# One load of the first tokens, issued as two transfers of 16 and 112 partitions

## The chip, the cores and the metric

The kernel runs on one core of a Trainium2 chip. The metric is the device time of one execution in microseconds. The kernel before took 180.99 us (median of three runs, 180.95 to 182.24 us).

A core has five instruction streams that run side by side and wait for each other on semaphores: TensorE (PE, the matrix multiplier), VectorE (DVE), ScalarE (ACT), GpSimd (POOL) and SyncE (SP). Transfers between the device memory and the on-chip memory are issued by SyncE, ScalarE or GpSimd, each on a queue of its own, and are carried out by 16 DMA engines that all queues share.

## The reference

Eight experts, each with its own 256 tokens, two weight matrices and two biases. All inputs are float32.

```
x: (8, 256, 512)   w1: (8, 512, 2048)   w2: (8, 2048, 512)   b1: (8, 2048)   b2: (8, 512)

h   = relu(matmul(x, w1) + b1)      # per expert: 256 x 2048
out = matmul(h, w2) + b2            # per expert: 256 x 512, float32
```

The weights are 4 MB for each of the 16 matrices in float32, and every one is used for 256 tokens only.

## The kernel before

**Data.** The kernel computes in float16. GpSimd's queue loads the weights and converts them on the way (`load`, line 88, called from `load_w1` and `load_w2`): one transfer for a matrix, except for the `w2` of the last two experts, which come in two halves. The tokens of experts 2 and 3 come in one transfer and those of experts 4 to 7 in another, on the same queue. Weights have room for three experts (`NW = 3`), so a later load waits until TensorE has finished with the one whose place it takes: for `s_ph` (first products of an expert done) or `s_po` (second products done).

**The tokens of experts 0 and 1** come another way. SyncE loads each as float32 into a tensor of its own, `x32[0]` and `x32[1]`, 128 partitions of 1024 elements (lines 131 and 132). Each partition holds two consecutive tokens, so a load is contiguous in device memory. VectorE casts expert 0 to float16 (line 133) and turns it with 32x32 block transposes into `xT` (function `transposes`, lines 121 and 124); ScalarE casts expert 1 (line 135). The two float32 tensors serve again at the end, as the places where the results of the last two experts are collected before SyncE stores them (line 246).

**Order before the section.** The lines up to 135 stand before a section that is synchronised by hand (line 138). In that first part the waits come from the framework, which tracks what each instruction reads and writes: the cast in line 133 waits for all transfers into `x32[0]`. SyncE's instructions of the first part are its x loads; in the section it first waits for what the first part leaves open. The issue of the first weights by GpSimd does not wait for any x load.

**The section.** SyncE is the gatekeeper (`go`, lines 240 to 242): it waits for the transposed tokens (`s_xT`) and for the landing of a weight load, and then raises `s_go`, on which TensorE waits. TensorE runs a loop of 11 steps (line 282). Step s computes the first product of expert s (line 292, 128 matmuls into four PSUM buffers, `ph`) and the second product of expert s - 3 (lines 319 and 309, into `po`). The page counts part of the matmuls of a group as one record. ScalarE adds the bias and applies the relu to each `ph` (line 226). For that it needs `b1T`, the transposed bias, which VectorE makes from rows that ScalarE has loaded (lines 129 and 191), between the transposes of expert 0 and those of expert 1. VectorE and ScalarE evict `po` (line 206).

**GpSimd's order** is: w1 of expert 0, b2, w1 of expert 1, tokens of experts 2 and 3, w1 of expert 2, w1 of expert 3, w2 of expert 0, tokens of experts 4 to 7, and from then on w1 and w2 in turn, w2 three experts behind. After the last weights come the stores of experts 0 to 3 and of 4 and 5; those of experts 6 and 7 are SyncE's.

Of the kernel before, what the change touches and what calls it, by code (L numbers as in the profile page):

```python
# [10 lines left out]
def kernel(  # L11
# [12 lines left out]
    nc = tc.nc  # L24
# [6 lines left out]
    P = 128  # L31
    nTB = T // P
# [15 lines left out]
    def sbuf(name, shape, dtype):  # L48
        return ctx.enter_context(nc.sbuf_tensor(name, shape, dtype))
# [14 lines left out]
    x32 = [sbuf(f"x32_{e}", [P, nTB, H], fp32) for e in range(2)]  # L64
# [39 lines left out]
    def transposes(e):  # L104
# [23 lines left out]
    tc.keep_in_program_order(nc.scalar.activation(out=warm[:], in_=ones1[:], func=relu))  # L128
    tc.keep_in_program_order(nc.scalar.dma_start(
        out=b1_rows[:], in_=b1.rearrange("e (b i) -> (e b) i", b=nB)))  # L130
    for e in range(2):
        nc.sync.dma_start(out=x32[e][:], in_=x[e].rearrange("(p tb) h -> p tb h", tb=nTB))
    nc.vector.tensor_copy(out=x16[0][0][:], in_=x32[0][:])  # L133
    transposes(0)
    tc.keep_in_program_order(nc.scalar.copy(out=x16[1][0][:], in_=x32[1][:]))  # L135
# [29 lines left out]
    def flush(first):  # L165
        n = GROUPS[first]
        for tb in range(nTB):
# [6 lines left out]
         in_=b2.rearrange("e h -> (e h)").rearrange("(o f) -> o f", o=1))  # L174
# [15 lines left out]
    for b in range(nB):  # L190
        turned = nc.vector.transpose(  # L191
            out=b1T[b * B : (b + 1) * B, nB - 1 - b : nB - 1 - b + nJ * B],
            in_=b1_rows[:].rearrange("r (i j) -> r j i", j=nJ),
# [23 lines left out]
    for s in range(E + LAG):  # L217
        if s < E:
# [3 lines left out]
            for j in range(nJ):  # L222
# [4 lines left out]
                    out=mine.rearrange("p (tb j k i) -> p j tb k i", tb=nTB, j=nJ, k=split)[:, j],  # L227
                    in_=ph[:, j % NPH, 0:T].rearrange("p (tb i k) -> p tb k i", tb=nTB, k=split),
# [19 lines left out]
    for s in range(E + LAG):  # L248
# [5 lines left out]
        e = s - LAG  # L254
# [112 lines left out]
```

## Time and profile before

| | |
|---|---|
| median of three runs | 180.99 us (180.95 to 182.24) |
| profiled execution, whole time | 181.05 us |
| its span, first to last instruction | 179.3 us |
| mean granted TensorE clock | 0.973 |
| busy: TensorE / VectorE / ScalarE / GpSimd | 133.7 / 86.8 / 75.5 / 12.5 us |
| read from device memory / written to it | 71.39 / 4.19 MB |
| the two x loads of SyncE, issue to landing | 3.4 and 4.5 us |
| first matmul | 16.14 us |
| last eviction begins | 173.13 us |

All times within an execution are counted from the start of the span. A row of a timeline gives the start, the duration, the engine and source line, the tile written and the one read, the number of instructions taken together, and in brackets the idle time before it with what ended it. "SPq" and "PEq" are the sequencers of SyncE and TensorE: issues and waits that are not counted as busy time. The queues are q0 (GpSimd), q1 (SyncE) and q10 (ScalarE). A transfer's time is from its issue to the moment when its semaphore shows that it has landed.

### The profile page before, as it was taken

How to read it: one execution, taken by the hardware profiler on the slowest of the kernel's cores; microseconds unless marked ns; L12 is line 12 of the kernel's file. 1: busy time of each engine (PE TensorE's matmuls, PEld its weight loads, DVE VectorE, ACT ScalarE, POOL GpSimd, SP SyncE). 2: the span in 40 equal slices, each digit the busy share in tenths (PEclk: the TensorE clock that was granted, in tenths of full speed). 3: DMA queues.
4: the chain of work that ended last, by engine and by line, in shares of the span. 5: the costliest groups of instructions: out<-in, count | busy, mean ns of one | idle time of the engine just before them, and what ended most of it. 6: DMA issues, size and time to landing. Idle time of an engine off the chain costs nothing. (4 is left out here: it accounts for less than half of the span.)

```text
span 179.3 us, 3015 instructions
## 1 busy us (share of the span) xinstructions
PE 133.7 (75%) x784; PEld 92.9 (52%) x784; DVE 86.8 (48%) x124; ACT 75.5 (42%) x153; POOL 12.5 (7%) x27
## 2 busy tenths in 40 slices
PE   0003979868699880998978896889699896999960
PEld 0003868858589330794468544874298333443420
DVE  0989938576000299998089906992320002031010
ACT  3201776757687113483097506780487111021010
POOL 6000011020200100001010001000200003010000
PEclk9999999999999998589999999999999999999996
DMA  5999999998999998999999999999989989999996
GB/s 209 273 194 218 234 194 218 234 219 190 236 223 190 230 230 190 223 234 216 194 234 223 194 227 230 208 205 234 219 190 234 223 190 223 210 212 221 316 424 261
DMA packets 3826, 40.46 MB, mean 226 GB/s; under 512 B 448, under 2 KB 464, under 8 KB 1136
## 3 DMA queue, kind: packets, MB, share of 16 engines
q0 software_dynamic: 3200, 38.28, 96.7%
q1 hardware_dynamic: 576, 2.10, 3.0%
q10 hardware_dynamic: 48, 0.07, 0.1%
q14 instruction: 2, 0.02, 0.0%
HBM read 71.39 MB, written 4.19 MB: 422 GB/s over the span
## 5 line engine op out<-in xcount | busy, mean ns | idle before, releaser
L292 PE MATMUL ph<-xT,w_sb 128*128 x512 | 72.2, 302 | 33.3 <-PEq L277 30.4
L292 PEld LDWEIGHTS ph<-xT,w_sb 128*128 x512 | 66.5, 145 | 40.1 <-issue 31.3
L226 ACT ACTIVATE hT<-ph,b1T 128x256 f16<-128x256 f32 x128 | 60.2, 474 | 33.4 <-PE ph L292 29.9
L124 DVE STREAM_TRANSPOSE xT<-x 32x256 f16<-32x256 f16 (+1 forms) x64 | 52.7, 893 | 25.2 <-DMA x<-in_x_dram 22.0
L309 PE MATMUL po<-w_sb,hT 128*128 x256 | 56.7, 379 | 2.2 <-issue 2.2
L309 PEld LDWEIGHTS po<-w_sb,hT 128*128 x256 | 24.9, 97 | 33.1 <-issue 7.1
L206 DVE COPY out<-po 32x512 f32<-32x512 f32 (+1 forms) x20 | 13.7, 687 | 42.9 <-PE po L309 42.6
L206 ACT COPY out<-po 32x512 f32<-32x512 f32 (+1 forms) x20 | 11.6, 578 | 46.0 <-PE po L309 45.8
L88 POOL DMA_DIRECT2D w_sb<-in_w_dram x18 | 9.7, 544 | 137.4 <-PE po L309 71.2
L121 DVE STREAM_TRANSPOSE xT<-x 32x256 f16<-32x256 f16 x32 | 14.0, 436 | 0.5
L206 DVE COPY x<-po 128x512 f32<-128x512 f32 x2 | 1.4, 692 | 14.0 <-PE po L309 14.0
L319 PE MATMUL po<-b_sb,ones 1*128 x16 | 4.8, 378 | 3.9 <-issue 2.5
L206 ACT COPY x<-po 128x512 f32<-128x512 f32 x2 | 1.2, 586 | 14.3 <-PE po L309 14.3
L319 PEld LDWEIGHTS po<-b_sb,ones 1*128 1x128 f16 x16 | 1.4, 90 | 6.6 <-issue 6.3
L191 DVE STREAM_TRANSPOSE b1T<-b_rows 32x512 f32<-32x512 f32 x4 | 4.1, 1023 | 0.5 <-issue 0.5
L135 ACT CAST x<-x 128x1024 f16<-128x1024 f32 x1 | 1.0, 1044 | 3.3 <-DMA x<-in_x_dram 3.3
L133 DVE CAST x<-x 128x1024 f16<-128x1024 f32 x1 | 0.7, 694 | 3.1 <-DMA x<-in_x_dram 3.1
L88 POOL DMA_DIRECT2D out_dram<-out x2 | 1.1, 538 | 9.5 <-DVE out L206 9.5
L128 ACT ACT_TABLE_LOAD x1 | 1.3, 1283 | 0.7 <-PEq L351 0.7
L88 POOL DMA_DIRECT2D x<-in_x_dram x2 | 1.1, 550 | 0.0
L127 DVE MEMSET ones<- 1x128 f16 x1 | 0.2, 165 | 0.9 <-PEq L351 0.9
L88 POOL DMA_DIRECT2D b_sb<-in_b_dram x1 | 0.5, 509 | 0.0
(5 smaller groups left out, 0.7 us busy)
## 6 DMA issues: line engine op xcount, KB each, us to landing
w_sb<-in_w_dram POOLq DMA_DIRECT2D x14, 2048.0 KB, 41.2
w_sb<-in_w_dram POOLq DMA_DIRECT2D x4, 1024.0 KB, 22.5
out_dram<-out POOLq DMA_DIRECT2D x1, 2048.0 KB, 25.1
x<-in_x_dram SPq DMA_DIRECT2D x2, 512.0 KB, 4.0
x<-in_x_dram POOLq DMA_DIRECT2D x1, 1024.0 KB, 34.5
out_dram<-out POOLq DMA_DIRECT2D x1, 1024.0 KB, 18.1
out_dram<-x SPq DMA_DIRECT2D x2, 512.0 KB, 7.0
x<-in_x_dram POOLq DMA_DIRECT2D x1, 512.0 KB, 24.5
```

Source lines behind the costliest of these rows:

```text
L88: engine.dma_start(**kw).then_inc(landed[key], 16)
L121: last = nc.vector.transpose(out=dst[:, :, g, :, 0, :], in_=block[:, :, :, 0, :])
L124: last = nc.vector.transpose(out=dst[:, tb, g], in_=block[:, tb])
L128: tc.keep_in_program_order(nc.scalar.activation(out=warm[:], in_=ones1[:], func=relu))
L133: nc.vector.tensor_copy(out=x16[0][0][:], in_=x32[0][:])
L135: tc.keep_in_program_order(nc.scalar.copy(out=x16[1][0][:], in_=x32[1][:]))
L191: turned = nc.vector.transpose(out=b1T[b * B : (b + 1) * B, nB - 1 - b : nB - 1 - b + nJ * B], in_=b1_rows[:].rearrange("r (i j) -> r j i" ...
L206: last = copy(out=results[e][at : at + rows, k * nTB + tb, :], in_=po[k * rows : (k + 1) * rows, bank : bank + H])
L226: nc.scalar.activation(out=mine.rearrange("p (tb j k i) -> p j tb k i", tb=nTB, j=nJ, k=split)[:, j], in_=ph[:, j % NPH, 0:T].rearrange("p ...
L292: last = nc.tensor.matmul(ph[:, j % NPH, 0:T], w1_sb[:, bass.ds(w_from + (kc * M + j), P, nJ)], xT[:, bass.ds(x_at + kc * T, T)], start=(k ...
L309: return nc.tensor.matmul(banks[tb], hT[:, bass.ds(h_from + (tb * nJ + j) * P, P)], w2_sb[:, bass.ds(w2_from + j * H, H)], start=False, st ...
L319: nc.tensor.matmul(banks[tb], ones1[:], b2_sb[:, bass.ds(s * H, H)], start=True, stop=False)
```

## The change

SyncE's first load is issued as two transfers: partitions 0 to 15 of `x32[0]`, then partitions 16 to 127. Both go on SyncE's queue, one after the other, ahead of the load of expert 1, which stays as it was. A partition's data is 4 KB, so the first transfer carries 64 KB and the second 448 KB. Nothing else in the source is changed; the cast in line 133 reads the whole tensor and so depends on both.

```diff
@@ -128,8 +128,8 @@
     tc.keep_in_program_order(nc.scalar.activation(out=warm[:], in_=ones1[:], func=relu))
     tc.keep_in_program_order(nc.scalar.dma_start(
         out=b1_rows[:], in_=b1.rearrange("e (b i) -> (e b) i", b=nB)))
-    for e in range(2):
-        nc.sync.dma_start(out=x32[e][:], in_=x[e].rearrange("(p tb) h -> p tb h", tb=nTB))
+    for e, p0, p1 in ((0, 0, 16), (0, 16, P), (1, 0, P)):
+        nc.sync.dma_start(out=x32[e][p0:p1], in_=x[e].rearrange("(p tb) h -> p tb h", tb=nTB)[p0:p1])
     nc.vector.tensor_copy(out=x16[0][0][:], in_=x32[0][:])
     transposes(0)
     tc.keep_in_program_order(nc.scalar.copy(out=x16[1][0][:], in_=x32[1][:]))
```

## The prediction

> **What bounds the kernel now.** I read the page's head and its parts 2 and 3 first: which engine is busy all the time?
>
> ```profile
> span 179.3 us, 3015 instructions
> DMA  5999999998999998999999999999989989999996
> q0 software_dynamic: 3200, 38.28, 96.7%
> q1 hardware_dynamic: 576, 2.10, 3.0%
> ```
>
> The DMA engines are at nine tenths in nearly every slice, and GpSimd's queue (q0) alone holds them for 96.7% of the span. SyncE's queue (q1), which the change touches, holds them for 3.0%: two x loads at the start, two stores at the end. Next the table by stretches (share of the 16 DMA engines and GB/s are the last two columns; six stretches from 6 to 168 us were asked, the first of these rows is the second of them), SyncE's waits between 131 and 150 us (total, times, longest), and the semaphore line of `go`.
>
> ```profile
> 20.00:50.00 30.00, 24.33 (x180) 22.69 (x178) 16.56 (x41) 20.97 (x46) 3.71 (x7) 1.00 1.02 216
> 140.00:168.00 28.00, 25.48 (x114) 10.97 (x113) 3.44 (x5) 2.90 (x5) 2.13 (x4) 1.00 1.01 212
> SPq L241 <- DMA w_sb<-in_w_dram: 19.2, 2, 9.7
> L242 SPq EVENT_SEMAPHORE  x18: 17/28/7361, 15.5 to 168.6; - x18
> ```
>
> The DMA share is 1.0 in these stretches, and a weight load lands every 9.6 to 9.7 us (19.2 us for two, 9.7 the longest; 9.66 below). So the weights are one unbroken stream, and the last piece is passed on to TensorE at 168.6 us. Is the stream ever short of issued work? GpSimd's issues answer that:
>
> ```profile
> 26.06 1.06 POOL L88 DMA_DIRECT2D w_sb<-in_w_dram  x2 [22.02 <-PE ph L292]
> 128.66 1.06 POOL L88 DMA_DIRECT2D w_sb<-in_w_dram  x2 [18.83 <-PE po L309]
> 148.03 1.05 POOL L88 DMA_DIRECT2D w_sb<-in_w_dram  x2 [18.31 <-PE po L309]
> ```
>
> When the last load goes out at 148.03 us, the one issued at 128.66 us still lies ahead of it, a whole load of 9.66 us: the stream has work ahead of it. Last, the chain of waits, in order of time:
>
> ```profile
> 109.30 39.43 DMA w_sb<-in_w_dram
> ...
> 165.92 7.19 PE po L309 x32
> 173.13 0.69 DVE x L206
> ```
>
> A load issued at 109.30 us lands 39.43 us later, at 148.73 us, because four loads' worth of stream lies before it. From there TensorE runs the last three second products back to back to 173.1 us, then comes the last eviction and store. **The end is therefore the start of the stream, plus its length, plus 24.4 us of TensorE and a store.** A change at the start can move the end in two ways only: by moving the stream, or by making TensorE late by more than it has to spare.
>
> **The change part by part.** The start as it is, with the issue times of SyncE's two loads (min/median/max, ns), SyncE's wait for the first weights, and the page's row of the x loads:
>
> ```profile
> 0.74 0.86 SPq L132 DMA_DIRECT2D x<-in_x_dram  x2
> 1.12 0.41 ACTq L129 DMA_DIRECT2D b_rows<-in_b_dram  x1
> 1.25 0.67 POOL L88 DMA_DIRECT2D w_sb<-in_w_dram  x1 [0.81 <-POOLq L351]
> 4.21 0.69 DVE L133 CAST x<-x 128x1024 f16<-128x1024 f32 x1 [3.13 <-DMA x<-in_x_dram]
> 4.94 7.18 DVE L121 STREAM_TRANSPOSE xT<-x 32x256 f16<-32x256 f16 x16
> 5.68 1.04 ACT L135 CAST x<-x 128x1024 f16<-128x1024 f32 x1 [3.34 <-DMA x<-in_x_dram]
> 12.60 4.13 DVE L191 STREAM_TRANSPOSE b1T<-b_rows 32x512 f32<-32x512 f32 x4 [0.49 <-issue]
> 16.14 9.62 PE L292 MATMUL ph<-xT,w_sb 128*128 x64 [16.14 <-PEq L277]
> 16.77 7.20 DVE L121 STREAM_TRANSPOSE xT<-x 32x256 f16<-32x256 f16 x16
> 17.29 0.47 ACT L226 ACTIVATE hT<-ph,b1T 128x256 f16<-128x256 f32 x1 [10.56 <-PE ph L292]
> L132 SPq DMA_DIRECT2D x<-in_x_dram x2: 382/404/425, 0.7 to 1.2; - x2
> SPq L241 <- DMA w_sb<-in_w_dram: 3.1, 1, 3.1
> x<-in_x_dram SPq DMA_DIRECT2D x2, 512.0 KB, 4.0
> ```
>
> *Added: one issue on SyncE.* 0.38 to 0.43 us, about 0.43 with the step to the next. The large part of x[0] and all of x[1] leave that much later. SyncE itself has time: it waited 3.1 us for the first weights after everything else.
>
> *Added: a later landing of x[0].* The cast starts at about 4.6 instead of 4.21 us, since it now waits for two transfers, and the first transposes end at about 12.5 instead of 12.1 us. What hides this is the first weight load, for which SyncE waits 3.1 us after those transposes. If x[0] were over 3.1 us late, TensorE's start at 16.14 us would move. The bias transposes end at 17.1 instead of 16.7 us; TensorE starts at 16.14 us into four buffers, so it runs on. x[1] is cast at 5.68 us and read by VectorE at 16.77 us: 10 us to spare.
>
> *Moved: the stream.* The bytes are the same, so it lengthens only by time in which DMA engines stand empty. How they start (share and GB/s last), and what each queue had moved by 4.6 us (first row) and by 5.2 us (the other two):
>
> ```profile
> 1.50:2.00 0.50, 0.00 (x0) 0.00 (x0) 0.00 (x0) 0.50 (x1) 0.50 (x2) 1.00 0.23 49
> 2.00:2.50 0.50, 0.00 (x0) 0.00 (x0) 0.00 (x0) 0.33 (x2) 0.50 (x2) 1.00 0.84 295
> 2.50:3.00 0.50, 0.00 (x0) 0.00 (x0) 0.00 (x0) 0.00 (x0) 0.50 (x2) 1.00 1.00 385
> q1 hardware_dynamic: 243, 0.93, 55.2%
> q1 hardware_dynamic: 288, 1.05, 54.8%
> q0 software_dynamic: 14, 0.23, 21.0%
> ```
>
> By 4.6 us q1 has moved 0.93 of 1.05 MB and q0 shows nothing; by 5.2 us the x loads are done and 14 weight packets show. So x goes first and the weights follow without a hole. Now the first part is an eighth of 512 KB, 64 KB; at 385 GB/s that is 0.17 us, and the second part follows 0.43 us after it. Unless something fills in, the engines stand empty for 0.43 - 0.17 = **0.26 us**, once. The bias rows, issued at 1.12 us on another queue, may fill part of it (also 64 KB, so down to 0.09). Behind the 448 KB part, 1.2 us of transfer, x[1] arrives in time, so there is no second hole. Upper bound: a whole issue, 0.43 us. Below nothing: the engines come in one by one (shares 0.23 and 0.84), 0.46 us lost in all; if a small transfer woke them sooner, perhaps half of that, 0.25 us, could come back, though the issue rows (0.41 us for the bias rows, 0.38 to 0.43 us for x) show no gain from a smaller transfer. I take 0.25 us, nearest to the hole as worked out.
>
> The Trainium skill, "DMA: Bandwidth & Descriptors", section "Rules for kernel authors", advises against two transfers to disjoint partition halves, because both spread over all 16 engines and so serialize; by it the change gains nothing, and the sum would be that of the second issue alone. The trace agrees that the x loads leave no engine idle to be won (share 1.00 at 2.5 us).
>
> **Sum:** the stream, and with it the landing at 148.73 us, moves by +0.25 us, and everything after it too. The profiled execution took 181.05 us (span 179.3 and 1.75 around it): 181.30. The median of the runs is 180.99 us, 0.06 less, so 181.24: I say **181.2 us**. The runs before spread from 180.95 to 182.24 us; one per cent, 1.8 us, is about what a measurement of this kernel can tell from no change.
>
> **The rivals.** *TensorE's reserve* decides two of them (TensorE's groups in order of time):
>
> ```profile
> 58.79 0.60 PE L319 MATMUL po<-b_sb,ones 1*128 x2 [0.49 <-issue]
> 72.06 9.74 PE L292 MATMUL ph<-xT,w_sb 128*128 x64 [5.32 <-PEq L277]
> 91.26 4.40 PE L292 MATMUL ph<-xT,w_sb 128*128 x32 [1.02 <-PEq L277]
> 110.62 4.40 PE L292 MATMUL ph<-xT,w_sb 128*128 x32 [1.62 <-PEq L277]
> 130.00 4.41 PE L292 MATMUL ph<-xT,w_sb 128*128 x32 [1.65 <-PEq L277]
> 149.12 0.60 PE L319 MATMUL po<-b_sb,ones 1*128 x2 [1.40 <-SPq L242]
> ```
>
> Before 72.06 us TensorE stands idle for 5.32 us, 4.3 more than the 1.02 us of a step without a wait; after that its gaps exceed that by 0.60, 0.63 and, where 0.5 us is usual, 0.9: 2.1 us in all.
>
> *Weights get in between (slower).* The engines could alternate between q1 and q0 once the first weight load's packets are there. It was issued at 1.25 us, and x's large part now comes 0.43 us later. A weight packet holds an engine for 9.66 / 8 = 1.21 us (128 partitions over 16 engines are 8 each). If each of the part's 7 packets per engine waited for one, x[0] would land 8.5 us late and more, 13.1 us. The bias transposes would end at 25.6 us, 8.3 us after ScalarE's first activation begins now (17.29), and expert 0 at about 34 instead of 25.8 us. With 10.3 to 10.9 us for each of the next three experts (two halves of 4.4 us, 0.5 between them, and a gap of 1.0 to 1.6) and 8.5 us for the first second product (0.5 + 0.6 + 0.3 + 7.1), TensorE would begin the work of 72.06 us 2.4 to 4.2 us late; 2.1 of that is taken up: 181.5 to 183.3 us, and 1.2 more if x lay behind all eight weight packets. It decides from about 8 us of lateness in x[0]. Against it: no weight packet shows by 4.6 us although that load had been issued since 1.92. If only x[1] is caught, its 10 us cover it. The Trainium skill, same page, section "Queues, rings and completion order", has each engine go round between the queues it has work for, packet by packet; by it this rival would be the rule, and the rows at 4.6 and 5.2 us do not bear that out for the start.
>
> *The second part held until the first has landed (slower).* The program might order the two as writes of one tensor. Landing takes some 3.5 us (issue 0.74, cast 4.21), so the large part would leave at 4.2 us; engines could be empty from 2.1 us until weights come, at the latest 4.6: up to 2.5 us, with the first rival's lateness on top: 182 to 185 us, taken at 183.5. Against: the rows written are disjoint.
>
> *Nothing, or a little less.* The hole is filled or the engines wake sooner: 180.8 to 181.0 us.
>
> *Faster by over 1%.* The stream would have to begin 1.8 us earlier, and it begins at 1.7 us; or its rate would have to rise, and it stands at share 1.0 throughout. Below 179.2 us; I see no mechanism and leave a small chance.
>
> **How the numbers follow.** Forecast, +0.1 to +0.45 us: 59%. Nothing or a little less: 18%. Weights between: 10%, six of it over 1%. Held until landed: 7%, six of it over 1%. Faster by over 1%: 6%. So faster 0.06, within one per cent 0.82, slower 0.12. The range from 180.5 to 182.7 us takes in both bounds of the hole, the spread upward of the runs before, and the milder half of the first rival; outside lie the worse rivals on both sides.
>
> **What would show it.** SyncE's three x issues from 0.74 to about 2.0 us; the cast at about 4.6 us; TensorE's start at 16.1 to 16.5 us; the step of 9.66 us per weight load unchanged; the landing that ends the long wait in the chain at about 149.0 instead of 148.73 us, and the last eviction that much later. A cast after 7.3 us would show a rival. The prediction is wrong if the step per load itself changes, or if TensorE's gap before the work at 149.12 us closes.

## The result, and the profile after

The changed kernel takes 181.81 us (median of 22 runs, 181.47 to 182.44) against 181.04 us (median of 22 runs, 180.78 to 182.46). The ratio is 1.0029, with a 95% interval from 1.0015 to 1.0042: between 0.27 and 0.76 us slower. The profiled execution took 181.77 us, 0.72 more than the one before (181.05). The median of 181.04 us, not the 180.99 of three runs, is used from here on. The ratios leave out one slow run, of 184.32 us, of the kernel with two halves further down.

The page's head and queues of the changed kernel:

```profile
span 180.0 us, 3017 instructions
DMA  6999999999999999999999999999999999999995
q0 software_dynamic: 3200, 38.28, 96.2%
q1 hardware_dynamic: 592, 2.10, 3.1%
```

Still one stream of weights. SyncE's queue has 16 packets more, one semaphore write for each DMA engine. Now the start of its timeline:

```profile
0.74 1.33 SPq L132 DMA_DIRECT2D x<-in_x_dram  x3
1.12 0.42 ACTq L129 DMA_DIRECT2D b_rows<-in_b_dram  x1
1.25 0.67 POOL L88 DMA_DIRECT2D w_sb<-in_w_dram  x1 [0.80 <-POOLq L351]
5.64 0.69 DVE L133 CAST x<-x 128x1024 f16<-128x1024 f32 x1 [4.56 <-DMA x<-in_x_dram]
6.36 7.18 DVE L121 STREAM_TRANSPOSE xT<-x 32x256 f16<-32x256 f16 x16
16.26 1.04 ACT L135 CAST x<-x 128x1024 f16<-128x1024 f32 x1 [13.92 <-DMA x<-in_x_dram]
17.74 4.19 DVE L191 STREAM_TRANSPOSE b1T<-b_rows 32x512 f32<-32x512 f32 x4 [4.20 <-ACT x L135]
```

There are three issues in 1.33 us instead of two in 0.86, as forecast. But x[0] is cast 1.43 us later than before, not 0.4, and x[1] at 16.26 instead of 5.68 us. VectorE's bias transposes, which I had taken to wait for x[0] alone, stand idle 4.20 us for ScalarE's cast of x[1]. SyncE, which releases TensorE, waits for x[1] too: 10.6 us for its load and 1.0 us for its cast. So TensorE starts late; its groups after that, and the chain of waits:

```profile
18.71 3.61 PE L292 MATMUL ph<-xT,w_sb 128*128 x16 [18.71 <-PEq L277]
73.05 9.55 PE L292 MATMUL ph<-xT,w_sb 128*128 x64 [2.43 <-PEq L277]
92.23 4.42 PE L292 MATMUL ph<-xT,w_sb 128*128 x32 [1.18 <-PEq L277]
111.64 4.40 PE L292 MATMUL ph<-xT,w_sb 128*128 x32 [1.67 <-PEq L277]
130.98 4.40 PE L292 MATMUL ph<-xT,w_sb 128*128 x32 [1.60 <-PEq L277]
150.14 0.60 PE L319 MATMUL po<-b_sb,ones 1*128 x2 [1.44 <-SPq L242]
```

```profile
110.27 39.48 DMA w_sb<-in_w_dram
...
151.00 8.76 PE po L309 x32
159.76 0.53 PE po L319 x2
160.29 7.01 PE po L309 x32
167.31 0.53 PE po L319 x2
167.84 7.03 PE po L309 x32
174.87 0.02 issue
174.89 0.69 DVE x L206
```

TensorE starts 2.57 us late (18.71 against 16.14), but the idle time before the fifth expert shrinks from 5.32 to 2.43 us and takes that up. TensorE still waits there, and from there on every group shown is 1.0 us later than before, and so is the landing that ends the long wait, at 149.75 us (110.27 + 39.48) against 148.73. The gap before the work at 150.14 us is 1.44 us, as good as the 1.40 before: TensorE still waits there for weights. **The lateness is the stream's, +1.02 us, where I had forecast +0.25.**

The end is less late than that. The second product at 151.00 us took 8.76 instead of 7.08 us in this execution, at a low TensorE clock:

```profile
152.00:154.00 2.00, 2.00 (x7) 0.71 (x5) 0.00 (x0) 0.00 (x0) 0.00 (x0) 0.55 1.03 213
154.00:156.00 2.00, 2.00 (x7) 0.78 (x6) 0.00 (x0) 0.00 (x0) 0.00 (x0) 0.59 0.96 201
```

The granted clock (third column from the end) was 0.55 and 0.59 there, and 1.00 in the same stretches before. The last eviction began 1.76 us later than before (174.89 against 173.13), and yet the span is only 0.7 us longer. Its last store, the shorter of SyncE's two (time from issue to landing, before and after), was 1.0 us quicker:

```profile
DMA to landing us min/median/max: 4.5/7.0/9.5
```

```profile
DMA to landing us min/median/max: 3.5/6.1/8.7
```

In both kernels it was issued while GpSimd's last store, issued at 159.08 and 161.78 us, was still under way. That one, too, landed quicker, at 177.2 and 177.9 us:

```profile
out_dram<-out POOLq DMA_DIRECT2D x1, 1024.0 KB, 18.1
```

```profile
out_dram<-out POOLq DMA_DIRECT2D x1, 1024.0 KB, 16.1
```

The DMA engines are full to the end in both: their share is 0.98 from 168 to 177 us, and their last data packet ends at 178.1 and 178.8 us, 1.2 us before the span does. So in this last stretch the time goes by the stores on the DMA engines, and 0.8 us more of TensorE there costs nothing. The same drop of the clock stands between 151 and 157 us in three profiles further down (112 + 16, x[1] by ScalarE, x[1] divided). In these and the changed kernel's the last eviction begins 25.0 to 25.2 us after the wait, in all others 24.3 to 24.4, and the time does not show it.

**Where the stream lost its microsecond.** One kind of row shows it: what each queue had moved by 4.8 us, first before, then after (packets, MB, share of 16 engines).

```profile
q1 hardware_dynamic: 261, 1.00, 56.7%
q10 hardware_dynamic: 48, 0.07, 3.7%
```

```profile
q1 hardware_dynamic: 160, 0.52, 34.1%
q0 software_dynamic: 15, 0.25, 23.9%
q10 hardware_dynamic: 48, 0.07, 12.1%
```

Two things changed. Weights (q0) have moved 0.25 MB while x[1] has not begun; and the same 48 packets of the bias rows (q10) have occupied the engines for 12.1% of 4.8 us, 0.58 us for each engine on average, instead of 0.18. By the trace's packet records, 8 of their 32 data packets took 0.68 to 0.93 us; before, none took over 0.12 us. The large part's first packet starts at 2.35 us, 0.59 us after the small part's. The stream does not make this good. The packets between 147 and 148.2 us, where "under 512 B" counts the engines that have finished the load of the long wait, before and then after:

```profile
DMA packets 29, 0.16 MB, mean 130 GB/s; under 512 B 13, under 2 KB 13, under 8 KB 13
```

```profile
DMA packets 20, 0.23 MB, mean 191 GB/s; under 512 B 4, under 2 KB 4, under 8 KB 4
```

Before, 13 of 16 engines had finished by 148.2 us and the other 3 before 149. After, 4 had by 148.2, 9 more by 149 and 3 after that. The first engine is 0.2 us late and the last a whole microsecond, and a load lands with its last engine. In the trace's completion records (one semaphore write for each engine) the last engine finishes 1.29 to 1.33 us after the first for every weight load that lands between 38 and 164 us, and 0.59 to 0.62 us in the kernel before. So the distance between the engines is made early and then stays.

The landing of the first weights is already 0.80 us late (16.08 against 15.28 us). The other 0.2 us comes between the loads that land at 28 and 38 us. One fetch of instructions (queue q14, 8 KB) holds one engine for 0.32 us there, in both kernels. That it met an engine which was already late in the changed kernel would fit, but the trace does not name the engine.

### The profile page after: what moved, and what is told of

It is laid out like the page before. It is cut to its first block, busy times and chain, and to the rows that moved or that the text cites. A ratio compares the mean times of both kernels' runs of the same rounds, so it can differ in the third digit from the quotient of the medians.

```text
span 180.0 us, 3017 instructions
## 1 busy us (share of the span) xinstructions
PE 135.5 (75%) x784; PEld 93.4 (52%) x784; DVE 86.9 (48%) x124; ACT 75.2 (42%) x153; POOL 12.5 (7%) x27
## 5 line engine op out<-in xcount | busy, mean ns | idle before, releaser
L309 PE MATMUL po<-w_sb,hT 128*128 x256 | 58.3, 387 | 1.6 <-issue 1.6
## 6 DMA issues: line engine op xcount, KB each, us to landing
x<-in_x_dram SPq DMA_DIRECT2D x1, 512.0 KB, 14.6
```

Source lines behind the costliest of these rows:

```text
L309: return nc.tensor.matmul(banks[tb], hT[:, bass.ds(h_from + (tb * nJ + j) * P, P)], w2_sb[:, bass.ds(w2_from + j * H, H)], start=False, st ...
```

## The experiments

The theories are these. **A**: the end follows the weight stream, which is late because the small part leaves a hole and the rest runs slower. **B**: any third issue on SyncE costs the same. **C**: the late x[1], through TensorE, makes the end late. Two came later. **D**: the bias rows fall into the hole and hold some engines. **E**: weight packets beside x packets run slower. All kernels are changes of the divided version or of the one before; this table has the profiled execution of each, and the ratio to the kernel before (four runs each for 112 + 16 and for the spare transfer, 9 to 22 for the others). "Wait ends" is the landing that ends the long wait in the chain; each kernel's rows follow further down where a verdict rests on them.

| kernel | cast of x[0], x[1] | TensorE starts | wait ends | its own time | ratio, 95% interval |
|---|---|---|---|---|---|
| before | 4.21, 5.68 | 16.14 | 148.73 | 181.05 | |
| changed (16 + 112) | 5.64, 16.26 | 18.71 | 149.75 | 181.77 | 1.0029, 1.0015 to 1.0042 |
| 64 + 64 | 11.18, 19.78 | 22.23 | 149.48 | 181.44 | 1.0027, 1.0017 to 1.0038 |
| 112 + 16 | 5.58, 18.12 | 20.57 | 151.32 | 183.23 | 1.0124, 1.0103 to 1.0145 |
| 16 extra, x[0] whole | 5.17, 17.57 | 20.02 | 150.63 | 182.61 | 1.0048, 1.0031 to 1.0064 |
| 16 + 112, x[1] by ScalarE | 6.58, 6.61 | 16.86 | 149.63 | 181.57 | 1.0020, 1.0008 to 1.0032 |
| 16 + 112, bias rows behind | 5.03, 15.99 | 18.55 | 149.34 | 181.30 | 1.0017, 0.9999 to 1.0035 |
| bias rows first, x[0] whole | 4.52, 16.51 | 18.96 | 149.56 | 181.55 | 1.0008, 0.9991 to 1.0025 |
| x[1] divided, not x[0] | 4.53, 17.46 | 19.92 | 150.73 | 182.93 | 1.0053, 1.0021 to 1.0084 |
| 16 + 112, weights later | 5.86, 6.89 | 17.19 | 150.19 | 182.12 | 1.0041, 1.0023 to 1.0059 |
| bias rows between the x loads | 4.22, 18.21 | 20.68 | 151.27 | 183.26 | 1.0060, 1.0027 to 1.0094 |
| both whole, bias rows behind | 4.00, 5.26 | 16.09 | 148.77 | 180.97 | 1.0001, 0.9985 to 1.0016 |

Read the fourth and fifth columns together: in every row the execution's extra time is 0.1 to 0.4 us less than the lateness of its wait. The third column has no such bond: TensorE starts at 22.23 us in one kernel and takes 181.44, at 17.19 in another and takes 182.12.

**Two halves.**

```diff
-    for e, p0, p1 in ((0, 0, 16), (0, 16, P), (1, 0, P)):
+    for e, p0, p1 in ((0, 0, 64), (0, 64, P), (1, 0, P)):
```

> x[0] divided into partitions 0 to 63 and 64 to 127. The first part (256 KB, about 0.6 us of transfer) covers the 0.43 us until the second follows, so there is no hole, and each DMA engine has 4 partitions of each part. Theory A (the stream is late because of the hole behind the small part and because 112 partitions, 7 for each engine, move slower per packet): the weight stream is not late, the long wait in the chain ends at 148.7 to 148.9 us, time within 0.2 us of the kernel before. Rival B (a third issue on SyncE costs by itself, whatever its size): the wait ends at about 149.7 us and the time is 0.5 to 0.8 us longer. Both: x[1] still leaves 0.43 us later than before; if that alone decides whether the weights get in between, ScalarE's cast starts near 16 us instead of 5.7.

Neither number came. The wait ends between the two theories, and something came that neither had: the second half of x[0] itself is caught among the weights, so that x[0] is cast at 11.18 us. There is more in this kernel than the sizes, too: each of SyncE's three issues took 0.55 to 0.59 us, x[1]'s as well, instead of 0.39 to 0.42, so they end at 2.55 instead of 2.07 us.

```profile
11.18 0.69 DVE L133 CAST x<-x 128x1024 f16<-128x1024 f32 x1 [10.10 <-DMA x<-in_x_dram]
22.23 3.60 PE L292 MATMUL ph<-xT,w_sb 128*128 x16 [22.23 <-PEq L277]
149.88 0.60 PE L319 MATMUL po<-b_sb,ones 1*128 x2 [1.43 <-SPq L242]
```

This is the prediction's rival, weights in between, for one half of x[0], and it shows that TensorE's reserve holds: with a start 6.1 us late, TensorE waits as long as ever (1.43 us) for the weights at 149.88 us. Theory C has little left.

**The large part first.**

```diff
-    for e, p0, p1 in ((0, 0, 16), (0, 16, P), (1, 0, P)):
+    for e, p0, p1 in ((0, 16, P), (0, 0, 16), (1, 0, P)):
```

> The same two parts, the 112 partitions first. No hole, since 448 KB cover the next issue. Theory A: only the slower packets of the 112-partition part are left; the slow engines lose about 0.5 us, the long wait ends at about 149.2 us and the time is 0.3 to 0.5 us longer than before. Theory A without slow packets (hole only): ends at 148.7 us, no longer than before. Rival B: as in the changed kernel, about 149.7 us and 0.5 to 0.8 us longer.

All three were too low: this is the slowest kernel of the study by the ratio, 1.24%, and 2.2 us by its own time. Without a hole, a whole 2.6 us of stream went. So the hole is not the only way to lose time, and not the largest. Where this went is taken up at the end of the section.

**A spare transfer ahead of the whole x[0].**

```diff
+    spare = sbuf("spare", [16, nTB, H], fp32)
+    nc.sync.dma_start(out=spare[:], in_=x[0].rearrange("(p tb) h -> p tb h", tb=nTB)[0:16])
     for e in range(2):
```

> x[0] whole, but ahead of it a 16-partition transfer of the same 64 KB into a spare tensor that nothing reads. The hole behind the small part is there, the packets of x[0] are 8 partitions for each engine as before, and 64 KB more are moved (0.17 us). Theory A: hole of 0.26 us and 0.17 us of extra bytes, so the long wait ends at about 149.1 us; the cast of x[0] about 0.5 us late. If instead the wait ends at 149.7 us, the 7-partition shares are not to blame and the hole or the issue is worth about 0.8 us. x[1] leaves 0.43 us late and is cast near 16 us if that decides.

The wait ends at 150.63 us, later even than in the changed kernel. Such a loss does not need shares of 7 partitions for each engine, then: x[0] was whole. And the bias rows are held here too, as the queue's row at 4.8 us says:

```profile
q10 hardware_dynamic: 48, 0.07, 12.7%
```

**x[1] out of the weights' way.**

```diff
+    tc.keep_in_program_order(nc.scalar.dma_start(
+        out=x32[1][:], in_=x[1].rearrange("(p tb) h -> p tb h", tb=nTB)))
     tc.keep_in_program_order(nc.scalar.dma_start(
         out=b1_rows[:], in_=b1.rearrange("e (b i) -> (e b) i", b=nB)))
-    for e, p0, p1 in ((0, 0, 16), (0, 16, P), (1, 0, P)):
+    for e, p0, p1 in ((0, 0, 16), (0, 16, P)):
```

> The change kept (16, then 112 partitions), but x[1] issued by ScalarE at 1.1 us, ahead of the bias rows, so that it is in the DMA engines' queues before the first weights. Theory A (x[1]'s late landing costs nothing at the end, the stream does): cast of x[1] at 5.5 to 6.5 us, TensorE starts at 16.1 to 17 us as before, and still the long wait ends at 149.2 to 149.8 us and the time is 0.3 to 0.8 us longer than before; the hole may be filled by x[1], which would bring it to the lower end. Rival C (the late x[1], through VectorE and TensorE, is what makes the end late): the time falls back to that of the kernel before.

As theory A has it: x[1] is in time, TensorE starts at 16.86 us, and the wait still ends 0.9 us late, with a time 0.08 to 0.32% longer than before.

**Weights later.** GpSimd issues b2 first, the first weights 0.63 us later (1.88 instead of 1.25 us).

```diff
-    load_w1(0)
     load(nc.gpsimd, "b2", out=b2_sb[:, LAG * H :],
          in_=b2.rearrange("e h -> (e h)").rearrange("(o f) -> o f", o=1))
+    load_w1(0)
```

> The change kept, but GpSimd issues b2 ahead of the first weights, which leave 0.51 us later (at 1.76 us). If the order of arrival decides who goes first, x[1] is then in the queues before the weights on the engines that finish x[0] first: cast of x[1] between 6 and 10 us and TensorE's start at 16.5 to 18 us. Theory A and D: the end hardly differs from the changed kernel (long wait ends at 149.4 to 149.9 us, 0.4 to 0.8 us longer than the kernel before), since hole and bias rows are as they were. Rival C: the time falls back to that of the kernel before.

```profile
6.89 1.04 ACT L135 CAST x<-x 128x1024 f16<-128x1024 f32 x1 [4.56 <-DMA x<-in_x_dram]
17.19 9.50 PE L292 MATMUL ph<-xT,w_sb 128*128 x64 [17.19 <-PEq L277]
```

Some half a microsecond decides who goes first: x[1] is cast at 6.89 us again. The end did not come back (0.23 to 0.59% longer), and the wait ends later than I had said (150.19 us). Part of that may be the edit itself: the first weight packet starts at 6.04 us, against 4.83 in the kernel before and 3.76 in the changed one. Theory C is out: in this kernel and the one before it TensorE starts within 1.1 us of its old time and the end is late all the same.

**The bias rows.** In the first kernel they are moved behind the x loads of the divided version, in the second ahead of the undivided x[0]; the third is the control, behind the x loads and nothing divided. In all three the issue by ScalarE is taken out; the cuts show the new one, and "..." stands for the unchanged source operand.

```diff
     for e, p0, p1 in ((0, 0, 16), (0, 16, P), (1, 0, P)):
         nc.sync.dma_start(out=x32[e][p0:p1], ...)
+    nc.sync.dma_start(out=b1_rows[:], in_=b1.rearrange("e (b i) -> (e b) i", b=nB))
```

> The change kept (16, then 112 partitions, then x[1]), but the bias rows issued by SyncE behind the x loads instead of by ScalarE at 1.1 us, so that they cannot enter the hole behind the small part. Theory D (in the changed kernel the bias rows fall into the hole and hold some DMA engines for 0.7 to 0.9 us with a single 2 KB packet, and these engines stay late for the whole stream): only the hole of about 0.3 us is left, the long wait in the chain ends at 149.0 to 149.2 us instead of 149.75, and the time is 0.1 to 0.3 us longer than that of the kernel before. Rival (the 112-partition part itself is slow): the wait still ends at about 149.7 us and the time is 0.5 to 0.8 us longer.

```diff
+    nc.sync.dma_start(out=b1_rows[:], in_=b1.rearrange("e (b i) -> (e b) i", b=nB))
     for e in range(2):
         nc.sync.dma_start(out=x32[e][:], ...)
```

> x[0] undivided; the bias rows issued by SyncE ahead of it, x[0] and x[1] 0.43 us later each. Theory D: the bias rows, first on idle engines, hold some of them as in the changed kernel, so these start x[0] late: the long wait ends at 149.4 to 149.8 us, the time is 0.5 to 0.8 us longer. Rival (the 112-partition part is slow): only a hole of about 0.3 us, the wait ends at 149.0 us, 0.1 to 0.3 us longer. x[1] is caught among the weights in both, cast near 16 us.

```diff
     for e in range(2):
         nc.sync.dma_start(out=x32[e][:], ...)
+    nc.sync.dma_start(out=b1_rows[:], in_=b1.rearrange("e (b i) -> (e b) i", b=nB))
```

> Control for the run with the bias rows behind the x loads: x[0] and x[1] undivided, the bias rows last on SyncE's queue. If moving the bias rows does nothing by itself, the long wait ends at 148.6 to 148.9 us and the time is within 0.2 us of the kernel before; x[1] is cast near 5.5 us and TensorE starts near 16.1 us. Then the 149.34 us of the divided version with the bias rows behind is the price of the division alone: hole and second start. If the wait ends at 149.3 us here too, that run says nothing of the division.

The control behaves like the kernel before (148.77 us, ratio 1.0001), so moving the rows is harmless by itself. It also has three issues on SyncE and loses nothing: theory B is out. With the rows out of the hole, the divided version's wait ends at 149.34 instead of 149.75 us: 0.41 of the 1.02 us goes with them, 0.61 stays. The engines finish closer together again: none of the 16 by 148.2 us, all of them before 149 (the row between 148.2 and 149 us).

```profile
DMA packets 33, 0.14 MB, mean 174 GB/s; under 512 B 16, under 2 KB 16, under 8 KB 16
q1 hardware_dynamic: 160, 0.52, 39.0%
```

But the second row, q1 by 4.8 us, has the same 160 packets as the changed kernel and 39.0% instead of 34.1% of the time: 1.87 against 1.64 us for each engine. What the bias rows no longer lose, the large part of x[0] loses in part. On average over the 16 engines the load lands 0.62 us late in the changed kernel and 0.55 us here: the bias rows mostly make the loss uneven, and the landing pays for the worst engine. Theory D is half right. Whoever comes after the hole starts slowly in these profiles, and in the changed kernel that is the bias rows; why it does is not shown. Bias rows first (149.56 us) lose 0.83 us of stream likewise, though the ratio (0.9991 to 1.0025) does not set that kernel apart from the one before. By the runs' ratios alone the price of the bias rows in the hole is not settled either: 1.0017 and 1.0029 have intervals that overlap. It rests on one profiled execution each.

**The late x[1] by itself.** The first divides x[1] instead of x[0]; the second puts the bias rows between two whole loads, so that x[1] leaves 0.47 us later (1.65 instead of 1.18 us) and nothing is divided; ScalarE's issue is again taken out. The latter was profiled three times.

```diff
-    for e, p0, p1 in ((0, 0, 16), (0, 16, P), (1, 0, P)):
+    for e, p0, p1 in ((0, 0, P), (1, 0, 16), (1, 16, P)):
```

> x[0] undivided and first; x[1] divided into 16 and 112 partitions instead. No hole (x[0] covers 1.2 us), the bias rows come behind x[0] as in the kernel before. The large part of x[1] leaves 0.43 us later and should be caught among the weights: cast of x[1] at 14 to 17 us, TensorE's start at 17 to 19 us as in the changed kernel. Theory A: the end does not notice, the long wait ends at 148.7 to 148.9 us, time within 0.2 us of the kernel before. Rival C (TensorE's late start is what costs): 0.5 to 0.8 us longer.

```diff
     for e in range(2):
         nc.sync.dma_start(out=x32[e][:], ...)
+        if e == 0:
+            nc.sync.dma_start(out=b1_rows[:], in_=b1.rearrange("e (b i) -> (e b) i", b=nB))
```

> x[0] undivided and first; then, on the same queue of SyncE, the bias rows, then x[1] undivided. x[1] leaves 0.43 us later than before, as in the changed kernel, and nothing else is disturbed: no hole, the bias rows behind x[0] as in the kernel before. It isolates the late x[1]. Theory A: x[1] is caught among the weights (cast at 13 to 17 us, TensorE starts at 17 to 19 us), and the long wait still ends at 148.7 to 149.0 us, time within 0.2 us of the kernel before. Rival C: TensorE's late start costs, 0.5 us or more. Rival E (weight packets that alternate with x packets take longer, and the engines on which that happens stay late): the wait ends at 149.3 us or later.

> The kernel with the bias rows between x[0] and x[1] once more, for a second profile: its executions lay between 180.9 and 183.3 us, and the one profiled was the slowest. Theory E (it is the slowing of weight packets beside x packets, different from execution to execution): x[1] is caught in every execution (cast at 13 to 19 us), and an execution that takes about 181 us shows the long wait ending near 148.8 us all the same. Theory F (the executions differ in whether x[1] is caught): an execution of about 181 us has the cast of x[1] near 6 us and TensorE's start near 16.1 us.

> The same kernel a third time, as above: by theory E the cast of x[1] lies at 13 to 19 us whatever the time, and the end of the long wait follows the time of the execution (about 148.8 us at 181 us, about 151.3 us at 183.3 us); by theory F the cast of x[1] follows it.

Here theory A fell as the only cause. With x[0] cast at 4.22 us, as before, and no division, the wait ended at 151.27 us in an execution of 183.26 us, 151.51 in one of 183.50 and 149.80 in one of 182.09. The ten timed runs spread from 180.88 to 183.26 us. x[1] was caught in all three profiles:

```profile
18.21 1.05 ACT L135 CAST x<-x 128x1024 f16<-128x1024 f32 x1 [15.88 <-DMA x<-in_x_dram]
151.66 0.60 PE L319 MATMUL po<-b_sb,ones 1*128 x2 [1.38 <-SPq L242]
```

```profile
16.73 1.04 ACT L135 CAST x<-x 128x1024 f16<-128x1024 f32 x1 [14.39 <-DMA x<-in_x_dram]
150.19 0.60 PE L319 MATMUL po<-b_sb,ones 1*128 x2 [1.37 <-SPq L242]
```

TensorE waits 1.38 and 1.37 us for the weights in both, so it is the stream again (theory E) and not TensorE. What weights and x did between 5 and 15 us, before, changed, and with the bias rows between (183.26 us):

```profile
q0 software_dynamic: 180, 2.22, 104.8%
```

```profile
q0 software_dynamic: 134, 1.90, 89.3%
q1 hardware_dynamic: 124, 0.48, 12.8%
```

```profile
q0 software_dynamic: 106, 1.72, 85.0%
q1 hardware_dynamic: 100, 0.41, 11.9%
```

In 85.0% of ten microseconds the last kernel moved 1.72 MB of weights, 105 packets of 16 KB: 16 engines x 8.50 us / 105 = 1.30 us each. The changed kernel: 16 x 8.93 / 116 = 1.23 us. So weight packets beside x packets do run slower, in some executions. The packet records say how many. Between 3 and 18 us, 30 of 169 weight packets took over 1.35 us in this execution and 1 of 167 in the changed kernel's. What they took over 1.23 us adds up to 0.65 us for each engine here, where the load of the long wait lands 1.01 us late on average over the engines. For 112 + 16 it is 0.82 of 1.49 us, so over half of that kernel's loss is of this kind; in the changed kernel it is 0.01 of 0.62 us. Theory E accounts for a part of what other kernels lose, then, and not for the change.

The division of x[1] gave the same picture, runs from 181.09 to 182.95 us. Theory F (that executions differ in whether x[1] is caught) has no support, though no execution of about 181 us came before the profiler. What makes the packets slow in one execution and not in another stays open.

None of the kernels is shown to be faster than the one before; the control equals it.

## Why the prediction was right or wrong

The time lies in the range (180.5 to 182.7 us), and "within one per cent" was the case that came. The size was too small by half: +0.25 us forecast, +0.27 to +0.76 measured. Part of the hit was luck: x[1] was caught among the weights, and in the changed kernel's profile the weight packets hardly slowed beside it, while in the four profiles that delay x[1] alone the wait ended 1.1 to 2.8 us late.

- **What bounds the kernel: right up to the long wait.** The step per load is unchanged, 9.69 us from the landing at about 110 us to the long wait's in both, and in all twelve kernels of the table the end goes with the landing of the long wait, not with TensorE's start. The last term of the sum, "24.4 us of TensorE and a store", does not hold as a path: 0.8 us more of TensorE there did not reach the end, which the stores on full DMA engines set.
- **"The engines stand empty for 0.26 us, once": the term that was mis-sized.** At the landing of the long wait it measured 1.02 us. I had priced the hole as idle time between two transfers at full speed. The trace shows a second start instead: the bias rows, which in my sum could only shrink the hole to 0.09 us, held the engines for 0.58 us on average instead of 0.18. Taking them away gave 0.41 us of the landing back and left 0.61 us. My upper bound, one issue of 0.43 us, was too low, and one hole was treated as if all 16 engines lost the same: they lost 0.62 us on average, and the load lands with the latest.
- **"10 us to spare" for x[1]: wrong.** I took its reader to be the transposes at 16.77 us. But the bias transposes, at 12.60 us before, already wait for its cast. It came 10.6 us later and they started 5.1 us later (17.74 us), so it had 5.4 us to spare; TensorE started 2.57 us late.
- **Weights in between: happened, to x[1].** I held against it that no weight packet showed by 4.6 us. That row could not bear this: x[1] had only just come first. When it left 0.47 us later the weights went ahead, and when these left 0.63 us later as well, x[1] was first again. The Trainium skill, "DMA: Bandwidth & Descriptors", section "Queues, rings and completion order", has an engine go round between the queues that have work; the trace agrees for x[1], which now lands 14.6 us after its issue instead of 4.5, and does not show it for the start of the kernel before.
- **TensorE's reserve: right.** The idle 5.32 us before the fifth expert took up the late start, and 6.1 us of lateness in the halves' kernel were taken up as well. The price that I gave the rival, 181.5 to 183.3 us, was not put to the test there: x[0] was cast 7.0 us late (11.18 us), short of the "about 8 us" from which it decides, and the median of 181.41 us comes with a stream that is late by itself.
- **Held until the first part had landed: did not happen.** The three issues follow one another from 0.74 to 2.07 us.

## What to carry to other kernels

In a kernel whose DMA queues never run dry, look for the moment at which each engine starts its part of the stream: in these profiles what an engine lost there it kept to the end, and every load landed with the latest engine. A small transfer ahead of a large one did not start the work sooner here; it made the engines start twice, and let other queues in between. Where two queues reach the engines within some half a microsecond of each other, the order can hang on one issue more or less on one of them.

## What the runs showed of the hardware that was not expected

- Behind a hole the bias rows were slow: their 48 packets took 12.1% and 12.7% of 4.8 us in two kernels with a hole, against 3.7% behind a running load. With the rows moved away, the 160 packets of x[0] took 39.0 instead of 34.1%.
- The engines of one stream did not draw together again: the last finished 1.29 to 1.33 us after the first for every weight load that landed between 38 and 164 us (0.59 to 0.62 us before), and 4 against 13 of 16 had finished the same load at 148.2 us.
- Weight packets of 16 KB that share the engines with 4 KB packets of another queue took 1.30 instead of 1.23 us on average in one execution; the executions of that kernel took 180.88 to 183.50 us.
- The granted TensorE clock fell to 0.55 and 0.59 in two stretches of 2 us in the middle of the back-to-back second products in the changed kernel's profile. In the one before it was 1.00 there. Between 70 and 78 us it fell to 0.50 in both.
- The three issues of SyncE in the kernel with two halves took 0.55 to 0.59 us each, against 0.38 to 0.43 in the kernel before and the changed one. No run gives the reason.
